# A routing table stored by blocks of eight keys, a sparse step moved between two DVE operations, an exponential issued later, squares moved to ScalarE

## The chip, the cores and the metric

One NeuronCore of a Trainium2 chip runs the whole program. The metric is the device time of one execution in microseconds (us), as the median of several runs. The engines are named as in the profile: PE (TensorE), DVE (VectorE), ACT (ScalarE), POOL (GpSimd) and SP (SyncE, which here only issues DMAs). "PEld" is PE's weight load, and a letter q behind an engine is its queue of issued DMAs.

## What is computed

Two layers of a transformer-like trunk over 256 context tokens and 256 latent tokens, 1024 wide, in fp32. Layer 0 mixes with attention, layer 1 with pooling and a bidirectional gated recurrence (RG-LRU). Each layer ends in the same expert network (PEER), which sets most of the time:

```python
q = (xc @ wq).reshape(PEER_CHUNK, PEER_HEADS, 2, PEER_HALF)
s = jnp.einsum('thpd,hpkd->thpk', q, subkeys)
s1, i1 = lax.top_k(s[:, :, 0], 16); s2, i2 = lax.top_k(s[:, :, 1], 16)
cand = s1[..., :, None] + s2[..., None, :]           # 16 x 16 candidates a head
cidx = i1[..., :, None] * 128 + i2[..., None, :]     # expert = 128 * i1 + i2
top_s, pos = lax.top_k(cand, 16)
g = jax.nn.softmax(top_s, axis=-1)
act = gelu(jnp.einsum('td,thkd->thk', xc, u[eidx]))
out = jnp.einsum('thk,thkd->td', g * act, v[eidx])
```

In the recurrence of layer 1, a = exp(-8 r softplus(-lam)), and the input is scaled by sqrt(1 - a^2), which the kernel works out as a root of (1 + a^2) times a tanh.

## The kernel before

The 16384 experts are 128 keys j of 128 experts i. The kernel doesn't gather experts for most tokens: it computes all of them. In a **key stage** (`peer`, first loop, with `u_step`) it loads the weights `uT` of one key (512 KB), splits them into a high and a low part (`load_split`: `whi` on ACT, `wlo` on POOL), multiplies them with all tokens in three matmuls per 128 channels (`mm3`), applies gelu on ACT (`gel`) and writes the result to DRAM (`Gd`). Beside it, a generator (`routing`, `route_tile`) makes the routing table for 128 tokens at a time: top 16 of the scores, of the candidates, softmax, and then, with one-hot matrices A and B and a matmul, a table of weights per expert i, key j and token t. `pace` runs this generator in step with the matmuls; every `yield` names a cost in units, and the units of all token tiles (93.5 for each, 52 for the last one of layer 0) are spread evenly over 112 keys in layer 0 and 120 in layer 1. In this loop the order on PE and DVE is the order in which the program writes it; ACT's and POOL's are the planner's.

The routing table goes from SBUF to DRAM in pieces of 16 tokens (`TG`): a staging tile `stg` of 128 experts x 128 keys x 16 tokens is filled by four ACT copies from PSUM and written to `Wd` by one DMA from POOL's queue (L962), 40 times in all, 1 MB each, a run of 8 KB in each partition.

In a **value stage** (`peer`, second loop, L1095 to L1133) the kernel goes through the 128 keys again. For every eighth key it loads the table of the next eight (`wb`, `JB` = 8) for all tokens through SP (L1098): 1.5 MB in layer 0 (384 tokens), 1 MB in layer 1, in runs of 512 B. For each key it loads `Gd` (`gr`) and the weights `vT`, splits the weights (`whi` on ACT, `wlo` on DVE), multiplies table and gelu on DVE (`G`, L1107), splits `G` (`gh` on ACT, `gl` on DVE; `split`, L351) and runs 24 matmuls over the 1024 channels (`v_mm`, L1167), which add up in PSUM.

The last 128 latent tokens of layer 0 take another way (`sparse`, L994): for each of their 128 chosen experts POOL gathers one value row per token and DVE adds it, scaled, to `ysp` (L1024). These 128 steps are spread over the keys 14 to 119 (S0, S1). In this loop the order on DVE and POOL is the program's. For each key it is: `wlo`, `G`, `gl`, then the sparse steps that are due.

In `route_tile`, the exponent `e` of the softmax is made on DVE (L910) and its exponential is issued on ACT right behind it (L911); the row sum of `e` (`z`) comes six wide DVE operations later.

The mixer of layer 1 is `rec_body`. Its order on PE and ACT is the program's, DVE's is the planner's. `decay` takes an exponential on ACT for each of 2 x 4 tiles, squares it on DVE (L1385) and multiplies (L1386); `root` takes the roots on ACT; `scan` runs the recurrence on DVE. The output projection is done in two halves (`w_half`); before the second half DVE makes the two last columns of `yq` (L1438, L1439), the input of the next layer norm's projection.

Of the kernel before, what the change touches and what calls it, by code (L numbers as in the profile page):

```python
# [8 lines left out]
F32 = mybir.dt.float32  # L9
# [5 lines left out]
AF = mybir.ActivationFunctionType  # L15
OP = mybir.AluOpType
# [5 lines left out]
P = 128  # L22
C = D // P
LC = 256
LL = 256
# [5 lines left out]
NK = 128  # L31
TOPK = 16
HEADS = 8
JB = 8
TG = 16
# [6 lines left out]
S0 = 14  # L42
S1 = 119
# [66 lines left out]
class Trunk:  # L110
# [767 lines left out]
    def route_tile(self, l, ps, rp, s, it, Wd):  # L878
        nc = self.nc
        V = nc.vector  # L880
# [27 lines left out]
        g = rp.tile([P, 3, HEADS, TOPK], F32, tag="g", name="g")  # L908
        e = g[:, 2]
        V.tensor_tensor(e, tv, tv[:, :, 0:1].to_broadcast([P, HEADS, TOPK]), op=OP.subtract)  # L910
        nc.scalar.activation(e, e, AF.Exp)  # L911
        sif = rp.tile([P, 16, TOPK], F32, tag="sif", name="sif")
        V.tensor_copy(sif, si)
        sifp = sif.rearrange("p (h x) k -> p h x k", x=2)
# [5 lines left out]
        for x in range(2):  # L920
            eq = rp.tile([P, HEADS, TOPK, TOPK], F32, tag="cand", name="eq")
            V.tensor_tensor(eq.rearrange("p h k j -> p (h k) j"),
                            abf[:, x].rearrange("p h k -> p (h k)")[:, :, None].to_broadcast([P, P, TOPK]),
                            self.iota[:, None, :TOPK].to_broadcast([P, P, TOPK]), op=OP.is_equal)
            yield 2.2
            V.tensor_tensor(eq, eq, sifp[:, :, x, None, :].to_broadcast([P, HEADS, TOPK, TOPK]), op=OP.mult)
            yield 2.2
            V.tensor_reduce(g[:, x], eq, axis=AX.X, op=OP.add)
            yield 2.2
        z = rp.tile([P, HEADS], F32, tag="z", name="z")  # L930
        V.tensor_reduce(z, e, axis=AX.X, op=OP.add)
# [19 lines left out]
        def flush(x):  # L951
            stg, A, B, u0, t0 = x
            for q0 in range(0, HB, 4):
                pw = ps.tile([P, 4, P], F32, tag="pw", name="pw")
                for t in range(4):
                    for y in range(2):
                        nc.tensor.matmul(pw[:, t], A[:, q0 + t], B[y][:, q0 + t], start=y == 0, stop=y == 1)
                q = u0 - t0 + q0
                nc.scalar.activation(stg[:, :, q:q + 4], pw.rearrange("p t j -> p j t"), AF.Copy, scale=1.0 / WSC)
                yield 1.36  # L960
            if u0 + HB == t0 + TG:
                nc.gpsimd.dma_start(Wd[it * (P // TG) + t0 // TG], stg)  # L962

        for t0 in range(0, P, TG):
            stg = rp.tile([P, NK, TG], F32, tag="stg", name="stg", bufs=2)
            for u0 in range(t0, t0 + TG, HB):
                A = rp.tile([P, HB, P], F16, tag="A", name="A", bufs=3)
                B = [rp.tile([P, HB, P], F16, tag=f"B{y}", name=f"B{y}", bufs=3) for y in range(2)]
                sh = [P, HB, P // 2, 2]
                x = [gT[:, y, u0:u0 + HB, None].to_broadcast(sh) for y in range(4)]  # L970
                io = self.iota16.to_broadcast(sh)
                Av, *Bv = (z.rearrange("p t (a b) -> p t a b", b=2) for z in (A, *B))
                V.tensor_tensor(Av, io, x[0], op=OP.is_equal)  # L973
                V.tensor_tensor(Bv[1], io, x[1], op=OP.is_equal)  # L974
                V.tensor_tensor(Bv[0], Bv[1], x[2], op=OP.mult)  # L975
                V.tensor_tensor(Bv[1], Bv[1], x[3], op=OP.mult)  # L976
                lag.append((stg, A, B, u0, t0))
                if len(lag) > 1:
                    yield from flush(lag.pop(0))
        for x in lag:  # L980
            yield from flush(x)
# [47 lines left out]
    def peer(self, l, t0, extra=None):  # L1029
        nc, a = self.nc, self.a  # L1030
        n = T - t0
        nd = n if l else n - P
        Wd = self.dram.tile([nd // TG, P, NK, TG], F32, name=f"Wd{l}")
        Gd = self.Gd[l]
        with ExitStack() as es:
            ps = self.pool(es, f"psU{l}", 2, PSUM)
# [48 lines left out]
        if l == 0:  # L1085
            sp = self.sparse(vp)
            done = -1
# [7 lines left out]
        for j in range(NK):  # L1095
            if j % JB == 0:
                wb = vp.tile([P, nd // TG, JB, TG], F32, tag="wb", name="wb")
                nc.sync.dma_start(wb, Wd[:, :, j:j + JB, :].rearrange("g i j t -> i g j t"))  # L1098
            g = vp.tile([P, nd], F32, tag="gr", name="gr", bufs=3)
            nc.sync.dma_start(g, Gd[j][:, :nd])  # L1100
            if l == 0 and j < XU:
                with self.tc.issue_after(self.gel.ins) if VG <= j < 6 else ExitStack():
                    nc.scalar.activation(g[:, :LC], g[:, :LC], AF.Gelu)
            with self.tc.issue_after(self.gel.ins) if j in VB else ExitStack():
                w = self.load_split(a["vT"][l, j])
            G = vp.tile([P, nd], F32, tag="G", name="G")
            nc.vector.tensor_tensor(G.rearrange("p (g t) -> p g t", t=TG), wb[:, :, j % JB, :],  # L1107
                                    g.rearrange("p (g t) -> p g t", t=TG), op=OP.mult)
            gh = vp.tile([P, nd], F32R, tag="gh", name="gh", bufs=3)
            gl = vp.tile([P, nd], F32R, tag="gl", name="gl", bufs=3)  # L1110
            if j < VD:
                nc.vector.tensor_copy(gh, G)
                nc.vector.tensor_tensor(gl, G, gh.bitcast(F32), op=OP.subtract)
            else:
                self.split(gh, gl, G)
            v = (w, gh, gl)
            if j < NK - KT:
                for d in range(C):
                    self.v_mm(y[d], v, d, 0, nd, j == 0)
            else:  # L1120
                last.append(v)
            if l == 0:
                if j in RC:
                    next(rc, None)
                if j == 40:
                    for d in range(C):
                        nc.vector.memset(y[d][:, nd:], 0.0)
                while done < (j - S0) * P / (S1 - S0):
                    if next(sp, 0) == 0:
                        break  # L1130
                    done += 1
                if j >= X0:
                    next(extra, None)  # L1133
        if l == 0:
# [158 lines left out]
    def rec_body(self, ps, rp, wk, h, tot):  # L1293
        nc, a, k = self.nc, self.a, self.rk
        V, G, A = nc.vector, nc.gpsimd, nc.scalar
# [83 lines left out]
        def decay(i):  # L1379
            for d in range(2):  # L1380
                x = d * 4 + i
                a_ = R[:, d, i]
                A.activation(a_, a_, AF.Exp, scale=k["nsp"][:, x:x + 1])
                a2 = self.w.tile([P, T], F32, tag="gel", name="a2", bufs=3)
                V.tensor_tensor(a2, a_, a_, op=OP.mult)  # L1385
                V.scalar_tensor_tensor(TH[:, d, i], a2, 1.0, TH[:, d, i], op0=OP.add, op1=OP.mult)  # L1386

        def root(i):
# [18 lines left out]
        for c in range(C):  # L1407
# [11 lines left out]
        pm = rp.tile([P, 2, 4, LL], F32R, name="pmix")  # L1419
        gg = rp.tile([P, 4, LL], F32, name="gg")  # L1420
        do = {"n": nxt, "c": conv, "m": lambda i: conv_mm((i,), 0, T), "g": gates, "p": pool, "o": pool_out, "d": decay,
              "r": root, "b": gate_branch, "s": scan}
        for x in MIX.split():
            do[x[0]](int(x[1:]))
        acc = [ps.tile([P, 2, LL], F32, tag=f"acc{i}", name=f"acc{i}", bufs=1) for i in range(4)]
        pmx = (pm[:, 0], pm[:, 1])
        for d in range(C):
            self.w_half(acc, 0, d, pmx)
# [2 lines left out]
            if d == 2:  # L1431
                rm = rp.tile([P, 2, 4, LL], F32R, tag="TH", name="rmix")
                for i in range(4):
                    V.tensor_tensor(gg[:, i], I[:, 0, i, LC:], gg[:, i], op=OP.mult)
                    self.split(rm[:, 0, i], rm[:, 1, i], gg[:, i])
        self.yq = yq = [x[:, :, :LL + 2] for x in self.h_tiles()]
        sh = self.mv[1][3][:, :, 1:2].to_broadcast([P, C, 2])
        V.tensor_copy(yq[0][:, :, LL:], sh)  # L1438
        V.tensor_tensor(yq[1][:, :, LL:], sh, yq[0][:, :, LL:].bitcast(F32), op=OP.subtract)  # L1439
        for d in range(C):  # L1440
            self.w_half(acc, 1, d, (rm[:, 0], rm[:, 1]))
            if d % 2 == 0:
# [1 line left out]
            x = self.XT[:, d, LC:]  # L1444
# [149 lines left out]
```

## Time and profile before

| | us |
|---|---|
| median of 3 runs (2859.86 to 2864.86) | 2862.78 |
| the profiled execution | 2869.51 |
| its span, first to last instruction | 2867.7 |
| key stage of layer 0, with its scores | 512 to 1255 |
| value stage of layer 0 | 1255 to 1855 |
| mixer of layer 1 | 1855 to 2060 |
| key stage of layer 1 | 2060 to 2502 |
| value stage of layer 1 | 2502 to 2851 |

Over the span PE is busy for 2652.9 us (93%), DVE for 2098.2 (73%), POOL for 1285.1 (45%), ACT for 1172.5 (41%), and the program moves 631.58 MB. An average like this hides the stages: what matters in each is how far its busiest engine is from its length, and what the waits in front of that engine end with. A stage table gives the first, the table of waits the second, and a timeline of one engine the beat of a loop.

### The profile page before, as it was taken

The page shows a single profiled execution, that of the slowest core. Times are in us where ns is not written, and L with a number is a line of the kernel's source. Part 1 is how long each engine was busy: PE and PEld are TensorE (multiplying, and loading weights), DVE is VectorE, ACT ScalarE, POOL GpSimd, SP SyncE. Part 2 cuts the span into 40 slices and gives each one's busy share as a digit, 9 for nine tenths or more (in the row PEclk, how much of TensorE's full clock was granted, in tenths as well). Part 3 has the DMA queues.
Part 4 walks back from the last instruction along what each step waited for, and adds up shares of the span by engine and source line. Part 5 has one row for each costly group of instructions (what it writes and reads, how often), then busy time and mean ns, then how long its engine had stood idle before and what let it go on. Part 6 is the DMA issues. An engine that isn't in the chain of part 4 may idle for free.

```text
span 2867.7 us, 45935 instructions
## 1 busy us (share of the span) xinstructions
PE 2652.9 (93%) x17403; PEld 2402.6 (84%) x17403; DVE 2098.2 (73%) x3697; ACT 1172.5 (41%) x1945; POOL 1285.1 (45%) x730
## 2 busy tenths in 40 slices
PE   8879999999899999999899998986999799999997
PEld 3667898987777777788888888976999799999997
DVE  5898764749958879226877777779839939677776
ACT  3444433433233333333333333354545445455544
POOL 3433430754444444445667665035387587600000
PEclk9989999999999999999999999998999999999999
DMA  7342262556547666667999998513477667898885
GB/s 258 125 133 74 95 211 81 192 190 242 197 169 269 228 227 221 196 235 259 316 324 340 342 322 305 190 50 111 157 217 242 210 209 240 289 302 294 293 287 167
DMA packets 296269, 631.58 MB, mean 220 GB/s; under 512 B 28480, under 2 KB 166384, under 8 KB 290416
## 3 DMA queue, kind: packets, MB, share of 16 engines
q1 hardware_dynamic: 226704, 468.03, 50.0%
q0 software_dynamic: 28768, 109.75, 10.3%
q10 hardware_dynamic: 40576, 50.87, 4.9%
q8 instruction: 136, 2.23, 0.3%
q14 instruction: 85, 0.70, 0.1%
HBM read 535.28 MB, written 93.33 MB: 219 GB/s over the span
## 4 chain that ended last, share of the span: by engine, by line
PE 47%; DVE 33%; issue 7%; DMA 6%; POOL 4%; ACT 3%; SPq 0%; ACTq 0%; DVEq 0%; POOLq 0%
PE y L1167 16%; PE pu L373 6%; PE pu L375 6%; PE pu L374 6%; DVE mj L166 4%; DVE A L973 3%; DVE B L975 3%; DVE B L976 3%; DVE wlo L365 3%; DVE B L974 2%; DVE ysp L1024 2%; POOL wlo L365 2%; PE pq L373 1%; PE pq L375 1%; PE pq L374 1%
## 5 line engine op out<-in xcount | busy, mean ns | idle before, releaser
L365 POOL TENSOR_TENSOR wlo<-wr,whi 128x1024 fp32r<-128x1024 f32 x306 | 800.7, 2623 | 729.3 <-ACT whi L364 591.9
L364 ACT ACTIVATE whi<-wr 128x1024 fp32r<-128x1024 f32 x575 | 609.1, 1060 | 937.6 <-PE pu L374 493.1
L1167 PE MATMUL y<-gh,whi 128*128 128x256 f32 (+1 forms) x2072 | 630.2, 310 | 41.4 <-ACT gh L352 40.1
L1167 PE MATMUL y<-gl,whi 128*128 128x256 f32 (+1 forms) x2072 | 642.6, 310 | 6.0 <-DVE gl L353 4.8
L1167 PE MATMUL y<-gh,wlo 128*128 128x256 f32 (+1 forms) x2072 | 637.7, 308 | 0.0
L365 DVE TENSOR_TENSOR wlo<-wr,whi 128x1024 fp32r<-128x1024 f32 x291 | 356.0, 1224 | 239.0 <-ACT whi L364 212.9
L1167 PEld LDWEIGHTS y<-gh,whi 128*128 128x128 f32 x2072 | 391.0, 190 | 52.6 <-ACT gh L352 50.5
L373 PE MATMUL pu<-hh,whi 128*128 128x512 f32 (+1 forms) x1024 | 395.7, 386 | 20.9 <-ACT gel L538 20.9
L1167 PEld LDWEIGHTS y<-gl,whi 128*128 128x128 f32 x2072 | 393.7, 190 | 15.3 <-DVE gl L353 12.8
L1167 PEld LDWEIGHTS y<-gh,wlo 128*128 128x128 f32 x2072 | 394.1, 190 | 0.0
L375 PE MATMUL pu<-hh,wlo 128*128 128x512 f32 (+1 forms) x1024 | 386.5, 377 | 3.7 <-POOL wlo L365 3.7
L374 PE MATMUL pu<-hl,whi 128*128 128x512 f32 (+1 forms) x1024 | 384.5, 375 | 0.0
L373 PE MATMUL pu<-h,whi 128*128 128x256 f32 x1024 | 296.1, 289 | 15.2 <-ACT whi L364 15.2
L375 PE MATMUL pu<-h,wlo 128*128 128x256 f32 x1024 | 290.6, 284 | 7.4 <-POOL wlo L365 7.4
L374 PE MATMUL pu<-h,whi 128*128 128x256 f32 x1024 | 289.6, 283 | 0.0
L373 PEld LDWEIGHTS pu<-hh,whi 128*128 128x128 f32 x1024 | 196.1, 191 | 53.4 <-ACT gel L538 22.7
L375 PEld LDWEIGHTS pu<-hh,wlo 128*128 128x128 f32 x1024 | 195.7, 191 | 41.0 <-POOL wlo L365 4.9
L374 PEld LDWEIGHTS pu<-hl,whi 128*128 128x128 f32 x1024 | 196.6, 192 | 31.8
L353 DVE TENSOR_TENSOR gl<-G,gh 128x384 fp32r<-128x384 f32 (+1 forms) x250 | 127.7, 511 | 119.6 <-ACT gh L352 119.6
L373 PEld LDWEIGHTS pu<-h,whi 128*128 128x128 f32 x1024 | 195.8, 191 | 15.4 <-ACT whi L364 15.4
L166 DVE SCALAR_TENSOR_TENSOR mj<-wm,cb 128x1024 bf16<-128x1024 f32 x128 | 206.6, 1614 | 1.0 <-DMA wm<-in_wmodT 0.8
L375 PEld LDWEIGHTS pu<-h,wlo 128*128 128x128 f32 x1024 | 195.2, 191 | 8.9 <-POOL wlo L365 8.9
(378 smaller groups left out, 4900.0 us busy)
## 6 DMA issues: line engine op xcount, KB each, us to landing
wr<-in_uT SPq DMA_DIRECT2D x278, 512.0 KB, 4.4
wr<-in_vT SPq DMA_DIRECT2D x256, 512.0 KB, 5.0
wm<-in_wmodT SPq DMA_DIRECT2D x80, 512.0 KB, 4.0
Wd<-stg POOLq DMA_DIRECT2D x40, 1024.0 KB, 7.0
Gd<-gel ACTq DMA_DIRECT2D x106, 256.0 KB, 2.4
wb<-Wd SPq DMA_DIRECT2D x16, 1536.0 KB, 12.5
gr<-Gd SPq DMA_DIRECT2D x128, 192.0 KB, 6.2
Gd<-gel ACTq DMA_DIRECT2D x172, 128.0 KB, 3.8
```

Source lines behind the costliest of these rows:

```text
L166: x = nc.vector.scalar_tensor_tensor(j, rs[i], 1.0, self.cb[:, s], op0=OP.mult, op1=OP.mult, accum_out=self.mv[l][n // C][:, n % C, s:s + 1])
L353: self.nc.vector.tensor_tensor(lo, x, hi.bitcast(F32), op=OP.subtract)
L364: nc.scalar.activation(hi, r, AF.Copy)
L365: (lo_engine or nc.vector).tensor_tensor(lo, r, hi.bitcast(F32), op=OP.subtract)
L373: nc.tensor.matmul(out, whi[:, s], hh[:, c, t0:t1], start=c == 0, stop=False)
L374: nc.tensor.matmul(out, whi[:, s], hl[:, c, t0:t1], start=False, stop=False)
L375: nc.tensor.matmul(out, wlo[:, s], hh[:, c, t0:t1], start=False, stop=c == C - 1)
L973: V.tensor_tensor(Av, io, x[0], op=OP.is_equal)
L974: V.tensor_tensor(Bv[1], io, x[1], op=OP.is_equal)
L975: V.tensor_tensor(Bv[0], Bv[1], x[2], op=OP.mult)
L976: V.tensor_tensor(Bv[1], Bv[1], x[3], op=OP.mult)
L1167: nc.tensor.matmul(y[:, n0:n1], w[:, s], g[:, n0:n1], start=first and x == 0, stop=False, skip_group_check=True)
```

## The change

Five edits:

- The routing table `Wd` is stored in DRAM as 16 blocks of eight keys; in a block, each expert row i has all tokens' pieces behind each other. A read of a block is then one run per partition (12 KB in layer 0, 8 KB in layer 1); the write of a staging tile, still one DMA from POOL's queue, becomes 16 runs of 512 B per partition.
- In the value stage of layer 0 the sparse steps come between `G` and the split into `gh` and `gl`.
- The exponential of the softmax is issued behind the first of the two row reductions, two yields of 2.2 units later.
- The square in `decay` is done by ACT (Square) and not by DVE.
- The two last columns of `yq` are made ahead of the first half of the output projection.

```diff
@@ route_tile
         V.tensor_tensor(e, tv, tv[:, :, 0:1].to_broadcast([P, HEADS, TOPK]), op=OP.subtract)
-        nc.scalar.activation(e, e, AF.Exp)
         sif = rp.tile([P, 16, TOPK], F32, tag="sif", name="sif")
...
             V.tensor_reduce(g[:, x], eq, axis=AX.X, op=OP.add)
+            if x == 0:
+                nc.scalar.activation(e, e, AF.Exp)
             yield 2.2
...
             if u0 + HB == t0 + TG:
-                nc.gpsimd.dma_start(Wd[it * (P // TG) + t0 // TG], stg)
+                nc.gpsimd.dma_start(Wd[:, :, it * (P // TG) + t0 // TG].rearrange("b i j t -> i b j t"),
+                                    stg.rearrange("p (b j) t -> p b j t", j=JB))
@@ peer
-        Wd = self.dram.tile([nd // TG, P, NK, TG], F32, name=f"Wd{l}")
+        Wd = self.dram.tile([NK // JB, P, nd // TG, JB, TG], F32, name=f"Wd{l}")
...
-                nc.sync.dma_start(wb, Wd[:, :, j:j + JB, :].rearrange("g i j t -> i g j t"))
+                nc.sync.dma_start(wb, Wd[j // JB])
...
             nc.vector.tensor_tensor(G.rearrange("p (g t) -> p g t", t=TG), wb[:, :, j % JB, :],
                                     g.rearrange("p (g t) -> p g t", t=TG), op=OP.mult)
+            while l == 0 and done < (j - S0) * P / (S1 - S0):
+                if next(sp, 0) == 0:
+                    break
+                done += 1
             gh = vp.tile([P, nd], F32R, tag="gh", name="gh", bufs=3)
...
-                while done < (j - S0) * P / (S1 - S0):
-                    if next(sp, 0) == 0:
-                        break
-                    done += 1
@@ decay
-                V.tensor_tensor(a2, a_, a_, op=OP.mult)
+                A.activation(a2, a_, AF.Square)
@@ rec_body
+        self.yq = yq = [x[:, :, :LL + 2] for x in self.h_tiles()]
+        sh = self.mv[1][3][:, :, 1:2].to_broadcast([P, C, 2])
+        V.tensor_copy(yq[0][:, :, LL:], sh)
+        V.tensor_tensor(yq[1][:, :, LL:], sh, yq[0][:, :, LL:].bitcast(F32), op=OP.subtract)
         pmx = (pm[:, 0], pm[:, 1])
         for d in range(C):
             self.w_half(acc, 0, d, pmx)
...
-        self.yq = yq = [x[:, :, :LL + 2] for x in self.h_tiles()]
-        sh = self.mv[1][3][:, :, 1:2].to_broadcast([P, C, 2])
-        V.tensor_copy(yq[0][:, :, LL:], sh)
-        V.tensor_tensor(yq[1][:, :, LL:], sh, yq[0][:, :, LL:].bitcast(F32), op=OP.subtract)
```

## Rows read from the trace of the kernel before

**Rows 1.** Busy us by stage: PE, PEld, DVE, ACT, POOL; clock, DMA share, GB/s

```profile
512.00:1255.00 743.00, 712.20 (x3864) 585.15 (x3862) 539.01 (x1105) 262.45 (x376) 353.81 (x150) 0.98 0.62 212
1255.00:1855.00 600.00, 553.24 (x3039) 533.62 (x3040) 446.89 (x563) 208.08 (x280) 340.56 (x259) 0.98 0.90 305
1915.00:2000.00 85.00, 60.11 (x365) 54.44 (x363) 75.80 (x84) 42.32 (x71) 47.09 (x30) 0.83 0.25 80
2060.00:2502.00 442.00, 408.31 (x3596) 401.85 (x3594) 316.84 (x449) 211.21 (x330) 335.58 (x142) 0.97 0.72 232
2502.00:2851.00 349.00, 348.97 (x3072) 348.61 (x3072) 254.83 (x388) 174.51 (x258) 0.00 (x0) 1.00 0.85 279
```

**Rows 2.** Waits, 1255 to 1855: total us, times, longest us

```profile
DVE gl L353 <- ACT gh L352: 119.6, 125, 6.2
...
PE y L1167 <- ACT gh L352: 40.1, 31, 5.1
```

**Rows 3.** Timeline of DVE, 1556 to 1564: start us, us, operation, idle before

```profile
1556.78 1.22 DVE L365 TENSOR_TENSOR wlo<-wr,whi 128x1024 fp32r<-128x1024 f32 x1
...
1559.12 0.60 DVE L353 TENSOR_TENSOR gl<-G,gh 128x384 fp32r<-128x384 f32 x1 [0.65 <-ACT gh L352]
1559.64 1.27 DVE L1024 SCALAR_TENSOR_TENSOR ysp<-hh,tot,ysp 128x1024 f32<-128x1024 f32 x1
1560.84 1.21 DVE L365 TENSOR_TENSOR wlo<-wr,whi 128x1024 fp32r<-128x1024 f32 x1
...
1563.69 2.59 DVE L1024 SCALAR_TENSOR_TENSOR ysp<-hh,tot,ysp 128x1024 f32<-128x1024 f32 x2
```

**Rows 4.** Chain that ended last, 1475 to 1500: start us, us, what

```profile
1481.98 16.85 PE y L1167 x95
```

**Rows 5.** DMA queues, 1171 to 1175: packets, MB, share of 16 engines

```profile
q1 hardware_dynamic: 1933, 1.27, 116.3%
```

**Rows 6.** DMA queues, 620 to 1140

```profile
q0 software_dynamic: 3456, 25.17, 12.3%
```

**Rows 7.** Timeline of SP, behind the table's load at 1555.90

```profile
1558.49 5.84 SPq L1100 DMA_DIRECT2D gr<-Gd  x1
```

**Rows 8.** Groups by line on POOL: busy us, mean ns

```profile
L962 POOL DMA_DIRECT2D Wd<-stg x40 | 23.0, 575 | 10.8 <-ACT stg L959 9.7 <-DMA Gd<-gel 0.9 <-issue 0.2
...
L137 POOL DMA_DIRECT2D cd<-cr x1 | 0.5, 510 | 3.0 <-ACT cr L135 3.0
...
L1009 POOL DMA_INDIRECT tot<-Gd,tot x128 | 152.1, 1188 | 56.2 <-issue 38.7 <-DVE gh L1112 17.5
```

**Rows 9.** Waits of ACT at the exponential, 512 to 1255, then 2060 to 2502

```profile
ACT g L911 <- DVE g L910: 34.0, 4, 13.6
...
ACT g L911 <- DVE g L910: 18.6, 2, 17.7
```

**Rows 10.** Waits of PE, 512 to 1255, then 2060 to 2502

```profile
PE pu L373 <- ACT gel L538: 20.9, 4, 8.1
...
PE pu L373 <- ACT whi L364: 15.2, 1, 15.2
```

**Rows 11.** Timeline of ACT, 937 to 943

```profile
937.48 1.06 ACT L364 ACTIVATE whi<-wr 128x1024 fp32r<-128x1024 f32 x1 [3.89 <-PE pu L374]
...
942.92 1.06 ACT L364 ACTIVATE whi<-wr 128x1024 fp32r<-128x1024 f32 x1 [3.89 <-PE pu L374]
```

**Rows 12.** Groups by line in the mixer, 1915 to 2000

```profile
L1385 DVE TENSOR_TENSOR a<-R 128x512 f32<-128x512 f32 x8 | 9.5, 1228 | 0.5 <-ACT R L1383 0.5
...
L1390 ACT ACTIVATE TH<-TH 128x512 f32<-128x512 f32 x8 | 4.9, 630 | 8.9 <-DVE TH L1386 8.9
```

**Rows 13.** Chain that ended last, 1980 to 1986

```profile
1981.43 2.28 DVE hh L1438
1983.73 2.30 DVE hl L1439
```

**Rows 14.** Groups by line, 2060 to 2502: DVE's one-hot matrix A

```profile
L973 DVE TENSOR_TENSOR A<-iota,gT 128x1024 f16<-128x1024 f16 x32 | 58.3, 1822 | 0.0
```

## The prediction

> **What bounds the kernel now.** I read the busy time by stage first [rows 1]. In it, look at how far PE is from the length of each stage, for that is all that an edit beside PE can win. The last expert stage (2502 to 2851) has 349.0 us of PE in 349 us: nothing that only shortens loads can help there. The first value stage (1255 to 1855) is 600 us long with 553 us of PE, so 47 us are open; the two key stages (512 to 1255, 2060 to 2502) have 31 and 34 us open; the mixer (1915 to 2000) has 25 us open, with DVE busy for 76 of 85 us. Then, for each of these, I read what PE and its feeders waited for.
>
> In the first value stage PE waits 40.1 us for ACT's gh [rows 2], which waits for G, which is DVE's. DVE is busy for 447 us and waits another 119.6 us for gh between G and gl [rows 2]; together that is 567 of 600 us. So DVE, counted with that wait, is the pacemaker, not PE. The steady beat shows it [rows 3]: from one wlo (1556.78) to the next (1560.84) are 4.06 us, of which 0.65 us is the wait in front of gl. There are 128 sparse steps in the keys 14 to 119, 1.22 a key, and an extra step costs 2.59 - 1.27 = 1.32 us, so the mean beat is 4.06 + 0.22 x 1.32 = 4.35 us. PE at full pace needs 16.85 us for 95 matmuls [rows 4], 24 x 0.177 = 4.26 us a key. DVE is late by little, but at every double step PE runs dry.
>
> **Sparse steps between G and gl.** DVE's order becomes wlo, G, sparse step, gl. The step lasts 1.27 us, longer than the 0.65 us that gh takes to arrive, so it covers the wait. On the 105 keys with a step DVE saves 105 x 0.65 = 68 us, and its beat falls to 4.35 - 0.65 = 3.70 us, below PE's 4.26. gl itself now ends 0.6 us later behind its G (1.27 instead of 0.65), but DVE can run ahead, with three gh and gl buffers. What queues behind a late row is new: a step that waits for its gathered row now holds the gl of its own key, before only that of the next. The bound above is all 47 us; the bound below is 0, if the gathers or the loads pace the stage (a rival). Gaps remain at the start, at the late rows and at the end, so I take well over half, **30 us**, together with the next part.
>
> **Routing table by blocks of eight keys, the read.** One load of the table for eight keys is 128 x 24 pieces of 512 B; afterwards it is 128 runs of 12 KB. On the DMA engines: in the 4 us in which little but these pieces moves [rows 5], 1933 packets fill 16 engines, 4 x 16 / 1933 = 33 ns each at most. Runs of 8 KB take 12.3% of 520 us x 16 for 25.17 MB [rows 6], 333 ns for each of 3072. So 14 loads fall from 14 x 3072 x 33 ns / 16 = 89 us to about 14 x 128 x 500 ns / 16 = 56 us, 33 us of the 541 us (0.90 x 600) that the stage has moving. And SP: the small load right behind the table's took 5.84 us to issue [rows 7]; the weights queued behind it start that much later, every eighth key. With 128 runs that stall should go. In the last stage the same saving is covered by PE and brings 0.
>
> The Trainium skill ("DMA: Bandwidth & Descriptors", Specifications) has 512 B as enough for line rate; by that rule the read saves nothing on the engines, and the 30 us would rest on DVE's order and SP alone, some 25. The trace differs: 318 GB/s for the pieces [rows 5], 393 GB/s (25.17 MB in 64 us of 16 engines) for runs of 8 KB [rows 6].
>
> **The write.** The same table is now written in 128 x 16 pieces of 512 B, 40 times, from POOL's queue. On the DMA engines: 2048 x 33 / 16 = 4.2 us instead of 128 x 333 / 16 = 2.7 us, 1.5 us more for each, 36 us in the first key stage and 24 us in the second, where the engines are at 0.62 and 0.72 [rows 1]: covered, 0. The staging tile has two buffers, so a write that lands 1.5 us later holds nobody up while POOL's next write is still being filled.
>
> POOL's own time to issue is the unknown. Now it is 0.575 us for 128 runs [rows 8]; 16 runs took 0.510 us, so a run adds (575 - 510) / 112 = 0.6 ns. By that, 2048 runs take 0.575 + 1920 x 0.0006 = 1.7 us. The other end is an indirect gather, 1.188 us for 128 rows, 9.3 ns a row, 19.0 us for 2048. A cheaper issue than today has no reason. I take the low end, for it is the same kind of instruction: 1.1 us more, 24 + 16 times. In the first key stage POOL has 354 of 743 us. In the second it has 336 us, of the 434 us that I expect for it: 18 us more fit, but wlo is POOL's too and PE already waits for it there now and then. **I charge 4 us** in all.
>
> The Trainium skill ("SBUF — State Buffer", SBUF: two separate sides) speaks against this: descriptors from GpSimd's queue can't be written while DVE holds the port that the two share. By it each write could also lose a DVE instruction's time; at the 1.8 us of DVE's A [rows 14] that is 16 x 1.8 = 29 us more of POOL in the second key stage, still inside its 98 us of room. The issue with 128 runs shows no such loss so far (mean 575 ns); no run here shows it for 2048.
>
> **The exponential.** ACT waits for e on DVE four times in the first key stage, 34.0 us, and twice in the second, 18.6 us [rows 9]; ACT's gel and whi are queued behind it, and PE waits for these: 20.9 us in four waits, and 15.2 us in one [rows 10]. The new place is two yields of 2.2 later. In the first stage 332.5 units of routing are spread over 112 keys, 2.97 units for a key of 5.44 us (942.92 - 937.48) [rows 11], so 4.4 units are 8.1 us. ACT's longest wait in this stage falls from 13.6 to 5.5 us, which the two PSUM buffers carry: of 20.9 us I take **17** (one of the four waits isn't at an exponential). In the second the shift is about the same, 17.7 becomes 9.6 us, and PE's 15.2 becomes 7: **8 us**. Bounds: 0 and 36 us for both. The next reader of e is the row sum on DVE, three wide operations after the new place; if ACT is late there, DVE waits, and its slack in these stages (539 of 743, 317 of 442 us) covers a few us.
>
> **Mixer.** Eight squares leave DVE: 9.5 us at 1.23 us [rows 12], in a stretch in which DVE hardly ever rests. ACT takes them at about the 0.63 us of its roots of that size, 5 us for the eight, in the stretch in which its roots already wait 8.9 us for DVE. DVE then waits for ACT's exponential and square in turn, so I take **4 us** of the 9.5. The bounds are the 9.5 us and a loss as large, should Square make ACT change tables or its chain become the longer one. The two small copies for yq stood on the path, 2.28 + 2.30 us [rows 13], before the residual on which ACT's next weights wait; they go ahead of the first half of the output projection, where they can fill a gap: **4 us**, between 0 (same chain, only earlier) and 4.6.
>
> **Sum.** The profiled execution took 2869.5 us (span 2867.7). 30 + 17 + 8 + 4 + 4 - 4 = 59 us less is 2810.5. It stands 6.7 us above the median of 2862.8, so the forecast is 2862.8 - 59 = **2804 us**.
>
> **Rivals.** (a) *DMA takes DVE's place in the first value stage.* For it: engines at 0.90 on average there, with gathers on one queue and weights on another. Against: 541 - 33 = 508 us of work, under PE's 553. If so the 30 us shrink to 10: 2824 us. (b) *Issuing pieces costs POOL in proportion to the 575 ns*, 4.5 ns a run, 9.2 us a write: the second key stage becomes POOL's, 336 + 16 x 8.6 = 474 instead of 434 us, with 5 us more in the first; in place of the 4 us that leaves a gain of 18: 2845 us. (c) *Slower: pieces cost what gathered rows cost*, 19 us a write. The second key stage becomes 336 + 16 x 18.4 = 630 us, 196 more than forecast, the first 354 + 24 x 18.4 = 796 instead of 726, 70 more: 63 - 266 = 203 us lost, about 3066 us. It decides from where POOL fills the second key stage, 0.6 + 98 / 16 = 6.7 us a write, and the whole is slower than before from about 10.5 us a write. For it: the only rows with many addresses are the gathers. Against: those read an index for each row. (d) *The edits move waits only*: ACT's order puts the exponential where it waits as before, late rows hold gl, the mixer's chain stays: within 8 us of before, 2858.
>
> **Chances.** Forecast 0.62, (a) 0.14, (b) 0.08, (c) 0.10, (d) 0.06. The range takes in (a) and (b), below it the full 47, 36 and 9 us where they come together in part: **2768 to 2850**; (c) and most of (d) are left out. About 0.2% (6 us) is what a measurement of this kernel can tell from none. Faster 0.87 (the forecast, (a), (b) and half of (d)), same 0.03, slower 0.10.
>
> **What would show it.** In the first value stage: DVE's wait for gh mostly gone, sparse steps directly behind G, PE's wait for gh under half of 40 us, and SP's 5.8 us issue gone. ACT's waits at the exponential under 10 us each, and PE's 15.2 us gap halved. The table's write on POOL near 1.7 us. In the mixer DVE's chain shorter by some us. Wrong would be: a write of over 6 us on POOL, with PE waiting for wlo in the second key stage; or a first value stage still near 600 us with the engines of DMA at 1.

## The result and the profile after

The changed kernel took 2811.45 us (median of 4 runs, 2805.92 to 2819.22) against 2863.82 us (median of 4, 2859.86 to 2868.17): a ratio of 0.982, 95% interval 0.9803 to 0.9836. It is faster by 52 us (1.8%); 59 were forecast. The profiled execution took 2819.22 us, span 2817.4 us. That the sum came out close is in part luck: the terms behind it did not.

The busy time by stage of the kernel after, to be laid beside [rows 1] (the second stage is taken here up to its last matmul; before, that stretch was 614 us with 567.24 us of PE):

```profile
512.00:1251.00 739.00, 708.06 (x3845) 581.80 (x3844) 538.32 (x1102) 260.73 (x371) 368.81 (x150) 0.98 0.64 213
1251.00:1815.00 564.00, 547.94 (x3161) 540.65 (x3160) 452.71 (x590) 213.66 (x293) 339.83 (x268) 0.99 0.89 326
1866.00:1951.00 85.00, 61.44 (x407) 57.72 (x407) 71.01 (x92) 47.05 (x82) 43.19 (x27) 0.86 0.33 106
2001.00:2441.00 440.00, 410.23 (x3597) 403.36 (x3595) 311.32 (x448) 211.23 (x328) 343.48 (x143) 0.97 0.74 232
2441.00:2803.00 362.00, 361.08 (x3062) 360.62 (x3063) 254.97 (x388) 174.19 (x257) 0.00 (x0) 1.00 0.79 270
```

Cut more sharply, from the first matmul of a stage to the first of the next, a value stage to the start of its last, the lengths in us are these, each of the profiled execution; the median is of all runs of the kernel. The key stage of a layer multiplies by the keys and the value stage by the values; the rows are the kernels of the experiments below.

| kernel | key 0 | value 0 | mixer | key 1 | value 1 | median |
|---|---|---|---|---|---|---|
| before | 743.1 | 614.0 | 190.2 | 442.2 | 348.8 | 2863.8 |
| after | 741.9 | 563.6 | 185.2 | 440.4 | 362.7 | 2811.5 |
| layout and squares alone | 740.1 | 591.7 | 186.2 | 440.6 | 362.0 | 2838.2 |
| order, exponential, copies alone | 742.1 | 578.5 | 190.6 | 441.9 | 348.8 | 2832.5 |
| after, exponential pinned late | 711.7 | 563.5 | 185.3 | 428.5 | 362.0 | 2772.2 |
| after, blocks of four keys | 741.0 | 562.8 | 184.4 | 452.6 | 348.6 | 2817.8 |
| after, once more | 741.8 | 561.8 | 184.8 | 439.2 | 348.6 | 2803.5 |
| pinned, blocks in layer 0 only | 711.5 | 564.9 | 184.5 | 422.3 | 348.8 | 2758.3 |

Three things stand out in the row of after: the first value stage won 50 us and not 30, the two key stages won next to nothing, and the last stage, in which nothing was expected to happen, lost 14 us.

**First value stage.** The waits in 1251 to 1815, total, times, longest; [rows 2] is their like before:

```profile
DVE wlo L365 <- ACT whi L364: 62.8, 71, 5.0
DVE gl L353 <- ACT gh L352: 31.9, 28, 4.1
```

and, of PE, in 1252 to 1815:

```profile
PE y L1169 <- ACT gh L352: 11.0, 10, 2.5
```

DVE's wait for gh fell from 119.6 to 31.9 us and PE's from 40.1 to 11.0. DVE now stands before wlo instead (26.5 us before): ACT's whi waits for a buffer that PE's y releases, so PE is the pacemaker. PE's stream shows it: the longest run of this stage's matmuls with no two starts 190 ns or more apart was 193 before and is 1351 now. DVE's timeline shows the steady beat, to be read against [rows 3]:

```profile
1553.64 1.23 DVE L365 TENSOR_TENSOR wlo<-wr,whi 128x1024 fp32r<-128x1024 f32 x1 [0.36 <-ACT whi L364]
1554.78 0.55 DVE L1109 TENSOR_TENSOR G<-wb,gr 128x384 f32<-128x384 f32 x1
1555.25 1.28 DVE L1026 SCALAR_TENSOR_TENSOR ysp<-vg,tot,ysp 128x1024 f32<-128x1024 f32 x1
1556.44 0.55 DVE L353 TENSOR_TENSOR gl<-G,gh 128x384 fp32r<-128x384 f32 x1
1557.80 1.22 DVE L365 TENSOR_TENSOR wlo<-wr,whi 128x1024 fp32r<-128x1024 f32 x1 [0.80 <-ACT whi L364]
```

The sparse step stands between G and gl, gl starts with no wait, and DVE idles 0.80 us a key in front of wlo. The beat, 1557.80 - 1553.64 = 4.16 us, is 24 matmuls at 0.173 us.

SP's queue behind the load of the table, the like of [rows 7], and then all of SP's issues of `gr` in the value stage, before and after, and of the weights, after (duration in ns, least, median and most):

```profile
1555.74 0.43 SPq L1100 DMA_DIRECT2D wb<-Wd  x1
1559.53 0.32 SPq L1102 DMA_DIRECT2D gr<-Gd  x1
...
L1100 SPq DMA_DIRECT2D gr<-Gd x123: 320/372/6448, 1259.3 to 1839.9; - x123
...
L1102 SPq DMA_DIRECT2D gr<-Gd x123: 319/335/1140, 1255.9 to 1786.4; - x123
...
L358 SPq DMA_DIRECT2D wr<-in_vT x122: 327/328/682, 1255.5 to 1781.8; - x122
```

Before, 13 of the 14 loads of `gr` right behind a load of the table took over 2 us to issue; after, all 14 took 0.32 to 0.33 us, and no issue of the weights took over 0.7. The stall is gone, as forecast.

**The write of the table on POOL**, the like of [rows 8]: 1177 ns instead of 575, for 2048 runs instead of 128.

```profile
L963 POOL DMA_DIRECT2D Wd<-stg x40 | 47.1, 1177 | 12.4 <-ACT stg L960 11.9 <-issue 0.5
```

**The exponential.** Waits of ACT at it, and PE's behind it, in the first key stage, then in the second; [rows 9, 10] are their like:

```profile
ACT g L929 <- DVE g L910: 34.5, 4, 13.6
...
PE pu L373 <- ACT gel L538: 21.1, 4, 8.1
...
ACT g L929 <- DVE g L910: 10.2, 2, 9.2
...
PE pu L373 <- ACT whi L364: 6.6, 1, 6.6
```

In the first key stage nothing moved (34.0 and 20.9 us before). In the second, both shrank, and the experiments show that it wasn't the edit that did it.

### The profile page after: what moved, and what is told of

It is laid out like the page before. It is cut to its first block, busy times and chain, and to the rows that moved or that the text cites. A ratio compares the mean times of both kernels' runs of the same rounds, so it can differ in the third digit from the quotient of the medians.

```text
span 2817.4 us, 46000 instructions
## 1 busy us (share of the span) xinstructions
PE 2644.6 (94%) x17403; PEld 2407.1 (85%) x17403; DVE 2080.1 (74%) x3689; ACT 1176.5 (42%) x1953; POOL 1300.8 (46%) x730
## 4 chain that ended last, share of the span: by engine, by line
PE 61%; DVE 25%; DMA 5%; issue 3%; ACT 3%; POOL 3%; SPq 0%; ACTq 0%; DVEq 0%; POOLq 0%
PE y L1169 26%; PE pu L373 7%; PE pu L375 7%; PE pu L374 7%; DVE mj L166 3%; DVE B L977 2%; DVE B L976 2%; DVE A L975 2%; POOL wlo L365 2%; DVE B L978 2%; DMA gr<-Gd 1%; PE pq L373 1%; PE pq L375 1%; PE pq L374 1%; PE pw L958 1%
## 5 line engine op out<-in xcount | busy, mean ns | idle before, releaser
L364 ACT ACTIVATE whi<-wr 128x1024 fp32r<-128x1024 f32 x575 | 608.7, 1059 | 905.3 <-PE pu L374 493.9
L1169 PE MATMUL y<-gh,whi 128*128 128x256 f32 (+1 forms) x2072 | 635.3, 309 | 12.8 <-ACT gh L352 11.0
L373 PE MATMUL pu<-hh,whi 128*128 128x512 f32 (+1 forms) x1024 | 394.8, 386 | 21.1 <-ACT gel L538 21.1
L374 PEld LDWEIGHTS pu<-hl,whi 128*128 128x128 f32 x1024 | 196.1, 192 | 31.6
L352 ACT ACTIVATE gh<-G 128x384 fp32r<-128x384 f32 (+1 forms) x250 | 115.6, 462 | 195.3 <-DVE G L1109 177.7
```

Of the source, the lines that this page charges most:

```text
L352: self.nc.scalar.activation(hi, x, AF.Copy)
L364: nc.scalar.activation(hi, r, AF.Copy)
L373: nc.tensor.matmul(out, whi[:, s], hh[:, c, t0:t1], start=c == 0, stop=False)
L374: nc.tensor.matmul(out, whi[:, s], hl[:, c, t0:t1], start=False, stop=False)
L1169: nc.tensor.matmul(y[:, n0:n1], w[:, s], g[:, n0:n1], start=first and x == 0, stop=False, skip_group_check=True)
```

## Experiments

### The two halves of the first value stage

Two kernels built on before. The first has the block layout (write, tile in DRAM, read) and the squares on ACT, and nothing else:

```diff
-        Wd = self.dram.tile([nd // TG, P, NK, TG], F32, name=f"Wd{l}")
+        Wd = self.dram.tile([NK // JB, P, nd // TG, JB, TG], F32, name=f"Wd{l}")
...
-                nc.sync.dma_start(wb, Wd[:, :, j:j + JB, :].rearrange("g i j t -> i g j t"))
+                nc.sync.dma_start(wb, Wd[j // JB])
...
-                V.tensor_tensor(a2, a_, a_, op=OP.mult)
+                A.activation(a2, a_, AF.Square)
```

> The kernel before with two of the five edits: the table by blocks of eight keys, and the squares on ACT. Theory (the value stage of layer 0 gained its 51 us by DVE's order): here the stage stays near 590 us (600 before, 549 after), DVE still waits about 115 us for gh in front of gl, and the whole is about 10 us faster than before. Rival (it gained them by the cheaper read of the table): the stage falls to 565 us or less and the whole is 35 us or more faster. The write of the table takes POOL 1.17 us, as after. Mixer: of the 5 us that it lost after, 3 to 5 are here if the squares did it, 0 to 2 if the copies for yq did.

The second has the other three edits: sparse steps between G and gl, the exponential's new place, the early yq copies. The first of them:

```diff
+            while l == 0 and done < (j - S0) * P / (S1 - S0):
+                if next(sp, 0) == 0:
+                    break
+                done += 1
             gh = vp.tile([P, nd], F32R, tag="gh", name="gh", bufs=3)
```

> The kernel after without those two edits: sparse steps between G and gl, the exponential issued later, the copies for yq early, but the table laid out and the squares done as before. Theory (DVE's order): value stage of layer 0 at 555 to 565 us, DVE's wait for gh at a third of 120 us or less, whole 40 us or more faster than before. Rival (the read): stage at 585 us or more, whole under 20 us faster. Key stage of layer 1: it is 439 us after, only 2.5 us less than before, although the gap at the exponential shrank by 8.5 us; if the longer write of the table gives back the difference, the stage is about 433 us here; if not, about 439 us.

Measured: layout and squares 2838.18 us (ratio 0.9907, 0.989 to 0.9923), order and the rest 2832.54 us (0.9891, 0.9874 to 0.9907). In the value stage the layout alone takes 22 us and the order alone 35.5, so neither of the two theories, that one edit did it all, holds. Together they take 50, so they overlap by 7; that is little more than the 5 us by which this stage differs between executions of one code (before 614.0, and 608.7 in the kernel with pauses below, which leaves this stage as it is; after 563.6, 561.8 and 558.4). The waits of DVE and PE with the layout alone, then with the order alone:

```profile
DVE gl L353 <- ACT gh L352: 101.0, 125, 3.8
...
PE y L1168 <- ACT gh L352: 25.0, 26, 5.1
```

```profile
DVE gl L353 <- ACT gh L352: 34.7, 27, 6.1
DVE G L1108 <- DMA gr<-Gd: 19.6, 11, 3.2
...
PE y L1168 <- ACT gh L352: 16.1, 10, 4.6
```

With the layout alone DVE keeps its 125 waits, and PE's fall all the same: SP's queue no longer holds up the loads (no issue over 1.6 us; ACT's wait for the weights' load went from 64.7 to 37.2 us), and the DMA engines are busy for 32 us less; no run parts these two. With the order alone DVE's wait for gh is mostly gone, but the old load of the table makes it wait 19.6 us for gr, the row behind that load on SP. Each edit removes a wait that the other leaves.

The mixer takes 186.2 us with the squares and 190.6 with the copies, against 190.2: the squares give 4 us, the copies nothing.

### What the exponential was worth

After, with one line around the exponential that pins it in ACT's queue behind the last gelu that the program has issued when it comes to it:

```diff
             if x == 0:
-                nc.scalar.activation(e, e, AF.Exp)
+                with self.tc.issue_after(self.gel.ins):
+                    nc.scalar.activation(e, e, AF.Exp)
```

> The kernel after with the exponential bound, in ACT's queue, behind the gelu that the program issued last before it, and so really late. Theory (the planner left the exponential in the key stage of layer 0 where it was, so that edit did nothing there): ACT no longer waits for e, PE's three gaps of 8.1, 7.0 and 3.9 us and the one of 6.6 us in layer 1 go; key stages 17 and 6 us shorter, the whole 20 us or more faster than after, about 2790 us. DVE then waits at the row sum for the exponential, in place of a later wait for PE's transposes. Rival (the gaps are DVE's lateness and only move): the stages stay within 4 us of after, with new PE waits at the transposes or at the table's matmuls.

Measured: 2772.18 us (ratio 0.968, 0.9653 to 0.9706), 39 us less than after; 20 or more had been expected. Why the edit of the change did nothing is seen in the order of ACT's instructions: in before and in after alike the six exponentials stand behind the 59th, 100th, 132nd, 161st, 346th and 404th weight split. ACT isn't in the program's own order here; a planner places its instructions, and a later line in the source left that place as it was (by what rule it chooses, no run shows). Pinned, they stand behind the 76th, 108th, 139th, 171st, 364th and 424th. The stages then, in the order of [rows 1], the two key stages:

```profile
508.00:1220.00 712.00, 700.28 (x3862) 577.15 (x3861) 537.04 (x1105) 263.40 (x377) 363.20 (x150) 1.00 0.66 222
...
1969.00:2397.00 428.00, 405.58 (x3593) 398.92 (x3591) 310.26 (x450) 211.49 (x330) 345.85 (x142) 0.99 0.77 239
```

and PE's waits in the first of them:

```profile
PE pw L959 <- DVE B L978: 4.7, 3, 3.4
PE pu L375 <- POOL wlo L365: 3.3, 5, 1.2
PE pu L373 <- ACT gel L538: 1.5, 1, 1.5
```

PE's wait for gel fell from 21.1 to 1.5 us, but the stage fell by 30. The rest is PE's busy time at a granted clock of 1.00 instead of 0.98: 708.06 to 700.28 us in these windows, and over the stage as cut in the table 710.3 to 700.0 us busy, 31.6 to 11.7 idle. Of the stage after, 34.1 us were granted at the lower level (1.2 GHz), of this one 3.4. In after, each of PE's four longest waits of this stage (8.1, 7.0, 3.9 and 3.4 us) has a drop that begins inside it and outlasts it. So a wait of PE here costs itself and, behind it, about half as much again (10.3 us busy for 19.9 idle); the prediction priced it at itself. The second key stage became 12 us shorter, its wait for whi gone.

### What the layout costs POOL

After, with blocks of four keys in place of eight (JB = 4): 4096 runs of 256 B for each write.

```diff
-JB = 8
+JB = 4
```

> The kernel after with blocks of four keys: 4096 pieces of 256 B for each write, 32 reads of 6 KB runs for each layer. If POOL's time to issue goes on as from 128 runs (0.575 us) to 2048 (1.177 us), 0.31 ns a run, it is 1.8 us here, and the key stages change by less than 5 us. If smaller pieces cost more each, it is 2.5 us or more, and the key stage of layer 1 grows by 5 us or more. The value stages stay within 5 us of after.

Measured: 2817.81 us (ratio 0.984, 0.982 to 0.986), and the group of the write:

```profile
L963 POOL DMA_DIRECT2D Wd<-stg x40 | 68.5, 1714 | 12.1 <-ACT stg L960 11.2 <-DMA Gd<-gel 0.6 <-issue 0.3
```

128 runs 575 ns, 2048 runs 1177 ns, 4096 runs 1714 ns: (1177 - 575) / 1920 = 0.31 ns a run, then (1714 - 1177) / 2048 = 0.26. The low end of the prediction's bounds was the right one, and still twice too high; the price per row of the gathers has no part in it. The price of a write came as expected, the stages did not: the second key stage got 12 us longer, where less than 5 was expected, and the last 14 us shorter. In the key stage PE's wait for whi is 15.7 us, as long as before the change, though the exponential stands where it stood in after; why DVE is late by 9 us in one and not in the other stays open. That the last stage fell to 348.6 us was the first hint that its 14 us weren't a steady cost.

### The last stage: a cost of the layout, or a state of PE

In the last stage of after PE has no wait behind its first two matmuls, and is slower all the same. PE's groups by form in 40 us of it, of before (2540 to 2580) and of after (2480 to 2520):

```profile
L1167 PE MATMUL y<-gh,whi 128*128 128x256 f32 x119 | 32.9, 276 | 0.0
```

```profile
L1169 PE MATMUL y<-gh,whi 128*128 128x256 f32 x114 | 32.0, 281 | 0.0
```

119 against 114 in the same time, idle 0.0 in both, the granted clock 1.00 in both. From start to start it is 113.3 ns against 117.8 ns, for 3008 matmuls in a row; 3072 x 4.4 = 13.6 us is the loss. PE's matmuls are the same in the two kernels, in order and shape; the addresses of their operands are not on record. And the 48 last matmuls, which come behind two short breaks (0.26 to 0.31 us and 0.22 us from start to start), run at the other pace in each: 117.8 ns in before, 113.3 in after. That suggested a state into which PE falls when it restarts. The rival was that reading the new table costs PE 4.4 ns a matmul. Three kernels tell them apart. After once more, unchanged:

> The changed kernel once more, nothing edited. In its first profile the value phase of layer 1 ran 3008 matmuls in a row at 117.8 ns where before ran them at 113.3 ns, with no wait between them and the granted clock at 1.00. Theory A (the pitch is a phase that PE falls into when it restarts after a wait, and the layout only shifts the restart): another execution may show either pitch; 113.3 ns here (stage 349 us, not 363) would prove it, 117.8 ns would leave it open. Theory B (the new table in DRAM costs PE 4.5 ns a matmul through its reads): 117.8 ns again, stage 362 to 363 us.

After, and before, with 16 forced waits in that stage (DVE copies one column of an accumulator into the tile that it overwrites next, so the key's operands can't be ready early):

```diff
+            if l and j % 8 == 4:
+                nc.vector.tensor_copy(G[:, 0:1], y[C - 1][:, 0:1])
             nc.vector.tensor_tensor(G.rearrange("p (g t) -> p g t", t=TG), wb[:, :, j % JB, :],
```

> The changed kernel, with PE made to wait 16 times in the value phase of layer 1: at every eighth key DVE copies one column of the last accumulator into the tile that it then overwrites with the key's product, so that this key's operands can't be ready before PE has finished the key before. Nothing of the result changes. Theory A (phase after a restart): the stretches of 192 matmuls between the pauses run some at 113.3 and some at 117.8 ns, each stretch at one of them from its first matmuls to its last. Theory B (layout, contention): all stretches at 117.8 ns. The pauses themselves cost some 1.5 to 2.5 us each, 25 to 40 us in all, so the total is about 2840 to 2850.

> The kernel before with the same 16 pauses in the value phase of layer 1. Theory A: here too some stretches between pauses run at 117.8 ns, though the table has the old layout. Theory B: all stretches at 113.3 ns. Total about 2863 plus 25 to 40 us for the pauses, up to 14 us more where stretches are at 117.8.

After once more took 2803.51 us, its last stage 348.6 us, its matmuls at 113.3 ns from first to last but for a few at the two short breaks. The same group in 2480 to 2520 of it:

```profile
L1169 PE MATMUL y<-gh,whi 128*128 128x256 f32 x118 | 32.6, 276 | 0.0
```

With the pauses (2836.02 us) the pace changes within one execution. Six windows of 20 us, each inside a stretch between two pauses, columns as in [rows 1]:

```profile
2450.60:2470.60 20.00, 20.00 (x179) 20.00 (x178) 12.66 (x19) 9.38 (x13) 0.00 (x0) 1.00 0.84 287
2475.00:2495.00 20.00, 20.00 (x173) 20.00 (x172) 12.57 (x18) 8.96 (x12) 0.00 (x0) 1.00 0.80 274
2498.90:2518.90 20.00, 20.00 (x179) 20.00 (x178) 12.67 (x19) 9.38 (x13) 0.00 (x0) 1.00 0.84 275
2642.30:2662.30 20.00, 20.00 (x179) 20.00 (x178) 12.68 (x19) 9.38 (x13) 0.00 (x0) 1.00 0.82 279
2667.00:2687.00 20.00, 20.00 (x172) 20.00 (x171) 12.72 (x18) 8.96 (x12) 0.00 (x0) 1.00 0.79 268
2690.60:2710.60 20.00, 20.00 (x179) 20.00 (x177) 12.66 (x19) 9.38 (x13) 0.00 (x0) 1.00 0.82 281
```

179 or 172 to 173, and nothing between. Of the 15 full stretches of 182 matmuls, 10 run at a mean of 113.3 to 113.5 ns and 5 at 117.76 ns, each from its first matmuls to its last; the lower DMA share in the slow ones (0.79, 0.80) fits the pace, since the transfers are the same for each key. PE at a restart, with a pause between a fast stretch and a slow one (the slow one begins behind a second, short break, at 2473.80):

```profile
2470.78 0.28 PE L1171 MATMUL y<-gl,whi 128*128 128x256 f32 x1
2470.89 0.28 PE L1171 MATMUL y<-gh,wlo 128*128 128x256 f32 x1
2472.55 1.18 PE L1171 MATMUL y<-gh,whi 128*128 128x256 f32 x8 [1.38 <-ACT gh L352]
2473.80 0.39 PE L1171 MATMUL y<-gl,whi 128*128 128x256 f32 x1
2474.02 0.28 PE L1171 MATMUL y<-gh,wlo 128*128 128x256 f32 x1
```

In before with the same pauses (2894.01 us) the 15 full stretches all run at 113.3 to 113.4 ns, and the last 48 matmuls again at 117.8. I had expected slow stretches there too, and there are none but the last. The theory of the restart stands, for one kernel shows both paces in the same stage, in two executions and, with the pauses, within one; the rival, that the new layout costs PE 4.4 ns a matmul throughout, falls.

What is left of the rival is that the layout moves the odds of a slow restart, and the tally speaks for it. With layer 1's table in blocks the last stage was slow in three of five executions without pauses (after, layout and squares alone, pinned; not with blocks of four, not in after once more) and in 5 of the 15 stretches; with the old table in layer 1 it was slow in none of three (before, order and the rest, the kernel of the next section) and in none of the 15 stretches. The old table is no guard against the pace as such, for the last 48 matmuls were slow in three of its four executions. What sets the odds is open.

### Blocks in layer 0 only

If the last stage gains nothing from the layout, layer 1 only pays for the write. So: the pinned exponential, and the old table in layer 1 (the write and the read follow the table's shape).

```diff
-        Wd = self.dram.tile([NK // JB, P, nd // TG, JB, TG], F32, name=f"Wd{l}")
+        Wd = self.dram.tile([nd // TG, P, NK, TG] if l else [NK // JB, P, nd // TG, JB, TG], F32, name=f"Wd{l}")
```

> The changed kernel with the exponential pinned behind the late work as in the run that did so (2772 us), and the block layout for layer 0's table alone: layer 1 writes and reads its table as before. Theory B (layout slows PE in the value phase of layer 1): that stage goes from 362 to 349 us, the POOL write of layer 1 back to 0.57 us, total about 2759. Theory A (phase of PE after a restart): the stage shows 349 or 362, whichever, and it isn't the layout that decides. Either way V0 stays at 563 us and the key phase of layer 0 at 712.

Measured: 2758.3 us (2756.83 to 2760.01; ratio 0.9628, 0.959 to 0.9666), the fastest of all, 53 us below after. The last stage was at 113.3 ns, which by the runs above can be the restart's doing and proves nothing on the layout. The second key stage went from 428.5 to 422.3 us, with the writes back at their old price:

```profile
L967 POOL DMA_DIRECT2D Wd<-stg x24: 1170/1171/1256, 627.2 to 1099.7; - x24
L965 POOL DMA_DIRECT2D Wd<-stg x16: 572/574/646, 2086.5 to 2370.3; - x16
```

(duration in ns, least, median and most). The 16 writes save 16 x 0.6 = 9.6 us of POOL, and the stage 6.

## Why the prediction was right, and where it was wrong

The forecast was 59 us below 2869.5; the profiled execution came out 50.3 below it. By terms:

| term | forecast | measured | how known |
|---|---|---|---|
| order and read, first value stage | -30 | -50 | both halves alone, and together |
| exponential, first key stage | -17 | -1 | ACT's order unchanged; pinned it is -30 |
| exponential, second key stage | -8 | -2 | the edit does nothing there either; pinned it is -12 |
| squares | -4 | -5, with the copies | stage with either alone |
| copies | -4 | 0 | the same |
| POOL's write | +4 | about +6 in layer 1 (inside the -2 above), 0 seen in layer 0 | layer 1 with the old table |
| last stage | 0 | +14 | state of PE after a restart; what part the layout has in it is open |
| ahead of the first stage, and the end | 0 | -6 | not pursued |

**The first value stage: the mechanism was right, the size too small.** What the prediction took from the bound of 47 us was PE's idle time, and that came out as it said: 614 - 567.24 = 46.8 us idle before, 564 - 547.94 = 16.1 after, 31 us less. The other 19 us are PE's busy time, 567.24 to 547.94. The step that failed is that the prediction held the 553 us of [rows 1] to be fixed. Away from breaks the stage's matmuls (128x384) start 173.3 ns apart in before and in after alike, and what PE is busy beyond that pace has two parts. With fewer waits the clock stays up: 27.3 us of the stage were granted at the lower level before, 6.8 after, which cost 12.8 and 3.4 us. And at the full clock PE starts slowly behind a wait (as above at 2473.80, where the next matmul comes after 0.22 us): starts 190 ns or more apart were 117 before and are 34 now, most of them within three matmuls of a wait, and cost, beside the idle time, 15.3 and 5.4 us. The two differences, 9.4 and 9.9 us, are the 19. So "the bound above is all 47 us" was no bound. The pace of 173.3 ns also makes PE's full pace 4.16 us a key: the prediction's 4.26 took in a slow start and a break among the 95 matmuls of [rows 4] and the length of the last. DVE was late by 0.19 us a key and not by 0.09.

**The read of the table.** The whole of the stage before, and with the layout alone:

```profile
1255.00:1869.00 614.00, 567.24 (x3161) 547.45 (x3161) 457.43 (x590) 214.24 (x293) 348.61 (x268) 0.98 0.88 299
```

```profile
1252.00:1843.00 591.00, 560.32 (x3161) 541.71 (x3161) 458.60 (x590) 213.36 (x292) 350.54 (x268) 0.99 0.86 310
```

0.88 x 614 = 540 us of the DMA engines became 0.86 x 591 = 508, 32 us less for the same bytes, with 33 forecast; a run of 12 KB took 493 ns in after, with 500 estimated. The table's own packets give 27 of the 32 (43008 pieces at a mean of 30.3 ns, 1792 runs at 488); the rest came from shorter times of the other packets, so the near match is in part chance. The Trainium skill ("DMA: Bandwidth & Descriptors", Specifications), by which pieces of 512 B already reach line rate, would have left this at zero; the runs side with the trace of before. SP's stall was to go, and went.

**The exponential: the fourth rival, in one place.** The step that failed is "the new place is two yields of 2.2 later". It counted the shift in the program's order, and ACT's order in this loop is the planner's, as the description of the kernel before has it. The profile of before could have raised the doubt: the 13.6 us wait shows ACT sitting at an instruction whose input was far off. What the removal of these waits is worth was also put too low: pinned, the two key stages gained 30 and 12 us, with 17 and 8 forecast and 36 as the upper bound for both. In the second key stage the wait for whi did fall to 6.6 us, as forecast, but with the layout alone it is 6.6 as well, and with the exponential's edit alone 15.2:

```profile
PE pu L373 <- ACT whi L364: 6.6, 1, 6.6
```

```profile
PE pu L373 <- ACT whi L364: 15.2, 1, 15.2
```

(waits of PE in the second key stage, layout and squares alone, then order, exponential and copies alone). A row that turns out as predicted didn't confirm the reason. The stage kept only 2 of these 8.6 us; 4 went into longer waits of pw for DVE's B (10.6 us before, 14.7 after), which are 12.5 and 10.3 in the two kernels with the old table in layer 1.

**POOL's write** was sized from two rows, 16 and 128 runs, and extrapolated sixteenfold; the estimate of 1.7 us stands against 1.18. The third rival, the price of gathered rows, was off by a factor of 16, and the second by 8. The Trainium skill ("SBUF — State Buffer", SBUF: two separate sides) has GpSimd locked out of writing descriptors while DVE runs an operation in a 2-port mode; the prediction took DVE's A for one, which no row shows. The 40 writes took 1170 ns at least, 1170 at the median and 1265 at most, so no row shows such a wait here. On the DMA engines the write is cheaper than the 33 ns a piece of the prediction: in 620 to 1140 of after,

```profile
q0 software_dynamic: 6528, 25.17, 16.1%
```

6528 packets, where [rows 6] has 3456 for the same bytes, and not 24 x 2048: each write went out in 256 packets of 4 KB, eight pieces in one.

**The last stage** was put at zero since PE fills it. PE does fill it, in both states. No row of before shows the second state but the 48 matmuls at its very end. The four runs of after, 2806 to 2819 us, spread as widely as the state is worth; that it is the reason was not seen in them, for only the profiled one (2819 us) has a trace.

**The net.** +20 us in the value stage, -16 and -6 in the key stages, -14 in the last one: the errors cancelled. A range built on the rivals held the time, though of the rivals only the fourth named any part of what happened, the exponential.

## What to carry to other kernels

Before costing a move in the source, find out who orders that engine's queue; where a planner does, ask whether the edit changes the planner's inputs, and pin the instruction if it must move. Price a wait of TensorE with what follows it, the slow restart and the granted clock, and don't take its busy time for a constant. Before explaining a loss in a stage that the change doesn't touch, run the same kernel again and compare the pitch of its matmuls.

## What the runs showed of the hardware

- PE ran the same 128x256 fp32r matmuls, with no wait between them, at 113.3 or at 117.8 ns from start to start, at the same granted clock (1.00), with the pace fixed at a restart and kept for up to 3008 matmuls.
- With PE's waits for gel cut from 21.1 to 1.5 us in a key stage, the time granted at 1.2 GHz fell from 34.1 to 3.4 us and the stage by 30 us.
- POOL's issue of one plain DMA took 575, 1177 and 1714 ns for 128, 2048 and 4096 runs, some 0.3 ns a run; its 512 B pieces left in packets of 4 KB.
- SP took over 2 us (up to 6.4) to issue a 192 KB load in 13 of the 14 places right behind a load of 3072 runs of 512 B, and 0.32 to 0.33 us in all 14 behind the same load in 128 runs.
- A wait of PE cost more than its idle time: in the first value stage the slow starts and the lower clock behind the waits came to 28 us before and 9 after, beside 47 and 16 us idle.
